# Hybrid decoder block on one core: seven-product gate and up tiles that sum in one PSUM bank

## Chip, cores and metric

One core of a Trainium2 chip runs the whole program in one launch. The metric is the device time in microseconds (us). TensorE (PE) does the matmuls, VectorE (DVE) and ScalarE (ACT) work beside it, GpSimd (POOL) does a little, and SyncE (SP) issues nearly all transfers. Results of matmuls land in PSUM, which has eight banks; everything else on the chip lives in SBUF.

## The reference

A decoder block on 512 tokens, with 16 learned tokens ahead of them (528 in all), model width 1024, in float32. A feed-forward network, a token mixer (latent attention and a gated DeltaNet out of one input projection), a second feed-forward network and a last norm:

```python
def swiglu(x, w_gate, w_up, w_down):
    return (jax.nn.silu(x @ w_gate) * (x @ w_up)) @ w_down
...
h = h + 0.5 * swiglu(rmsnorm(h, ffn1_norm[l]), ffn1_w_gate[l], ffn1_w_up[l], ffn1_w_down[l])
u = rmsnorm(h, mix_norm[l])
...
merged = jax.nn.sigmoid(gate_mla) * y_mla + jax.nn.sigmoid(gate_gdn) * y_gdn
h = h + merged @ w_out[l]
h = h + 0.5 * swiglu(rmsnorm(h, ffn2_norm[l]), ffn2_w_gate[l], ffn2_w_up[l], ffn2_w_down[l])
...
return rmsnorm(h, final_norm)[:, N_META:]
```

The hidden width of either network is 2816, which is 22 tiles of 128.

## The kernel before

Activations stand with the channels on the 128 partitions and the tokens along the row. A float32 product is made of three matmuls of the type fp32r: both sides are split into a high part (a cast by ACT: L173 for plain weights, L272 elsewhere) and a low part (the rest, a subtraction by DVE: L174, L273), and high x high, high x low and low x high are summed.

**The feed-forward networks** (`ffn`). The first six of the 22 hidden tiles are made by plain products, gate and up, "dense" in what follows (L188). The other 16 are made in pairs. For one pair and one of gate and up (a *quad*, j = 0 for gate and 1 for up; 16 quads per network, 32 in all) the two hidden tiles and the two halves of the tokens form a 2 x 2 block product, which is computed with seven instead of eight block products (the Winograd form of Strassen's method). `quad` loads the two raw weight tiles (512 KB each, in a pool of four), makes four sums of weight blocks on DVE (`side`, L394), splits each of the seven weight operands (`form`: 128x512 into one tile, high part in its first half and low part in its second, in eight slots of three kinds) and runs seven products (`product`, L405) of twelve matmuls each: four blocks of 128 channels times three. A matmul has 264 columns in FFN1 and 256 in FFN2. Every product has a PSUM bank to itself, from four small pools in the order of `BANKS`. After each product DVE adds it to a partial sum or to the output (`add`, L398; eight per quad); only the first product is copied by ACT (L421). The activation operands of the products, `xf`, are formed once per network.

The 22 hidden tiles stand in three chunks, `CHUNKS`: 0 to 8 (the six dense tiles and one pair), 8 to 16 and 16 to 22. In chunks 1 and 2 the down projections of the chunk before follow the quads: `down(c, m)` loads and splits one weight tile (L173, L174), runs 48 matmuls in FFN1 (two halves) or 24 of 512 columns in FFN2 (L188, tile `dn`), and DVE adds the result to the residual `hk` (L323). So chunk 1 is eight times quad and down, chunk 2 six quads with eight downs. At the end of a chunk, `halve` splits its hidden tiles for the downs to come (ACT cast into `ra`, L272). The downs of the last chunk follow at the end.

**The mixer** lies between the two networks. Its weights go through the same pool as the downs' (`wtiles`: `wraw`, `whi`, `wlo`, three slots each). What sets its order is a priority per part (`At`), by which a scheduler places the instructions on each engine.

**What sets the order around the change.** Each engine works through its own queue in the order that the scheduler wrote; it waits where an operand, or a slot that a tile is to reuse, is not ready. Products of a quad stand on PE in the order of the code: 1, 6, 2, 7, 5, 3, 4.

## Time and profile before

| what | us |
|---|---|
| median of three runs | 1211.47 |
| lowest, highest | 1210.93, 1213.09 |
| span of the profiled execution | 1213.2 |

The profiled execution is one more execution; its span lies 1.7 us above the median of the runs. Times in the views count from the start of that span. FFN1's dense tiles run until some 81 us, its quads until about 327 us and its last downs until 374 us; the mixer lasts until about 847 us; FFN2's quads follow from some 916 us, its last downs end about 1198 us. In a row of the views, L12 is line 12 of the kernel, `x84` a count of instructions, and "<-" in brackets names what ended the idle time ahead. PEclk is the clock that TensorE was granted, 1.00 being 2.4 GHz and 0.50 being 1.2 GHz.

### The profile page before, as it was taken

To read this page: it belongs to the slowest core of one execution; us is meant where nothing else is said; L and a number is where in the kernel's file an instruction comes from. 1 tells how busy PE (TensorE), PEld (TensorE's weight loads), DVE (VectorE), ACT (ScalarE), POOL (GpSimd) and SP (SyncE) were. 2 spreads that over 40 slices of the span, in tenths; PEclk is the share of its full clock that TensorE was granted. 3 is DMA by queue.
4 is the path that set the end of the run, shared out by engine and by line. 5 is a ranking of instruction groups with operands and counts; after the bars stand their busy time and mean duration, and the time that the engine had idled before them with its cause. 6 is when DMAs were issued, how large, how long until landed. Compare 5 with 4: busy or idle time off the path is not lost.

```text
span 1213.2 us, 20599 instructions
## 1 busy us (share of the span) xinstructions
PE 1182.6 (97%) x8094; PEld 1072.4 (88%) x8094; DVE 857.0 (71%) x1545; ACT 539.7 (44%) x922; POOL 127.1 (10%) x129
## 2 busy tenths in 40 slices
PE   7999999999999899999999999999999999999996
PEld 7999999999999789788897777788889999999985
DVE  7978777876656877784667665554979777786754
ACT  6544334533345553254425564434536433543443
POOL 1000000000011545020400000222000000000002
PEclk9999999999999888898999999999999999999998
DMA  6433233232244322245534544554642233233222
GB/s 233 143 103 100 94 105 105 88 118 75 88 138 138 126 61 81 81 145 149 162 101 142 173 132 135 169 185 141 199 157 88 90 103 104 94 106 115 79 78 70
DMA packets 68961, 145.37 MB, mean 120 GB/s; under 512 B 20000, under 2 KB 26480, under 8 KB 68864
## 3 DMA queue, kind: packets, MB, share of 16 engines
q1 hardware_dynamic: 68320, 143.52, 37.0%
q8 instruction: 64, 1.05, 0.3%
q10 hardware_dynamic: 544, 0.52, 0.1%
q14 instruction: 33, 0.27, 0.1%
HBM read 126.47 MB, written 17.55 MB: 119 GB/s over the span
## 4 chain that ended last, share of the span: by engine, by line
PE 86%; DVE 5%; issue 3%; POOL 2%; ACT 2%; DMA 2%; SPq 0%; DVEq 0%; POOLq 0%; ACTq 0%
PE gu L405 27%; PE dn L188 21%; PE gu L188 11%; PE gate L188 6%; PE wo L188 4%; PE mo L188 3%; PE qkv L188 2%; DVE wlo L174 1%; PE kk L804 1%; PE s L1085 1%; PE s L1082 1%; PE qk L943 1%; POOL rk L827 1%; DVE rk L827 1%; DVE T L829 1%
## 5 line engine op out<-in xcount | busy, mean ns | idle before, releaser
L173 ACT CAST whi<-wraw 128x1024 fp32r<-128x1024 f32 (+1 forms) x127 | 129.2, 1017 | 195.6 <-issue 65.3
L174 DVE TENSOR_TENSOR wlo<-wraw,whi 128x1024 fp32r<-128x1024 f32 (+1 forms) x127 | 155.8, 1227 | 26.2 <-ACT whi L173 25.5
L405 PE MATMUL gu<-hd,form 128*128 128x264 f32 (+1 forms) x1152 | 154.6, 283 | 0.0
L405 PEld LDWEIGHTS gu<-hd,form 128*128 128x128 f32 x1152 | 146.6, 190 | 1.3
L272 ACT CAST form<-sf 128x512 fp32r<-128x512 f32 x128 | 78.6, 620 | 126.1 <-DVE sf L394 67.5
L323 DVE SCALAR_TENSOR_TENSOR hk<-dn,hk 128x528 f32<-128x528 f32 (+2 forms) x49 | 33.7, 688 | 109.8 <-PE dn L188 109.6
L405 PE MATMUL gu<-ut,form 128*128 128x264 f32 x768 | 101.1, 284 | 0.0
L405 PE MATMUL gu<-rb,form 128*128 128x256 f32 x768 | 100.0, 283 | 0.0
L188 PE MATMUL dn<-hd,whi 128*128 128x264 f32 (+2 forms) x366 | 97.4, 319 | 0.0
L272 ACT CAST form<-wraw 128x512 fp32r<-128x512 f32 x96 | 59.3, 620 | 85.2 <-PE gu L405 52.1
L405 PEld LDWEIGHTS gu<-ut,form 128*128 128x128 f32 x768 | 96.5, 188 | 0.0
L405 PEld LDWEIGHTS gu<-rb,form 128*128 128x128 f32 x768 | 95.6, 192 | 0.0
L273 DVE TENSOR_TENSOR form<-sf,form 128x512 fp32r<-128x512 f32 x128 | 86.9, 683 | 11.2 <-ACT form L272 11.1
L188 PE MATMUL gate<-ut,whi 128*128 128x512 f32 x256 | 87.8, 417 | 0.0
L188 PE MATMUL dn<-ra,whi 128*128 128x264 f32 x464 | 85.3, 285 | 0.0
L188 PE MATMUL dn<-ut,whi 128*128 128x512 f32 (+1 forms) x238 | 83.6, 390 | 0.0
L235 POOL TENSOR_TENSOR sqa<-sq 128x512 f32<-128x512 f32 (+1 forms) x3 | 4.5, 1514 | 674.3 <-ACT sq L222 674.3
L188 PE MATMUL gu<-ra,whi 128*128 128x264 f32 x384 | 64.5, 290 | 7.4 <-ACT whi L173 6.6
L188 PE MATMUL dn<-ra,wlo 128*128 128x264 f32 x352 | 71.6, 285 | 0.0
L188 PE MATMUL dn<-ut,wlo 128*128 128x512 f32 (+1 forms) x182 | 70.4, 387 | 0.0
L273 DVE TENSOR_TENSOR form<-wraw,form 128x512 fp32r<-128x512 f32 x96 | 65.5, 684 | 6.7 <-ACT form L272 6.4
L188 PEld LDWEIGHTS dn<-ra,whi 128*128 128x128 f32 x464 | 68.5, 189 | 0.0
(435 smaller groups left out, 2480.7 us busy)
## 6 DMA issues: line engine op xcount, KB each, us to landing
wraw<-w SPq DMA_DIRECT2D x88, 512.0 KB, 3.3
wraw<-win SPq DMA_DIRECT2D x36, 512.0 KB, 3.5
wraw<-d SPq DMA_DIRECT2D x32, 512.0 KB, 3.8
wraw<-d SPq DMA_DIRECT2D x16, 384.0 KB, 3.2
hk<-xT SPq DMA_DIRECT2D x16, 264.0 KB, 3.6
dec<-growd SPq DMA_DIRECT2D x8, 512.0 KB, 5.8
gated<-gt SPq DMA_DIRECT2D x16, 256.0 KB, 2.2
sg<-gated SPq DMA_DIRECT2D x16, 256.0 KB, 2.8
```

Source lines behind the costliest of these rows:

```text
L173: ih = nc.scalar.copy(hi[:, 0:n], raw[:, 0:n])
L174: il = (nc.gpsimd if pool_lo else nc.vector).tensor_tensor(out=lo[:, 0:n], in0=raw[:, 0:n], in1=hi[:, 0:n].bitcast(F32), op=ALU.subtract)
L188: trail.append(nc.tensor.matmul(o, lhsT=w, rhs=x[:, lo_:hi_], start=start and k == 0 and pi == 0, stop=stop and k == n - 1 and pi == 2).ins)
L272: nc.scalar.copy(hi, x)
L273: (eng or nc.vector).tensor_tensor(out=lo, in0=x, in1=hi.bitcast(F32), op=ALU.subtract)
L323: nc.vector.scalar_tensor_tensor(out=o, in0=p, scalar=0.5, in1=o, op0=ALU.mult, op1=ALU.add)
L405: nc.tensor.matmul(ps, lhsT=wt, rhs=xt, start=k == 0 and i == 0, stop=k == 3 and i == 2)
L804: nc.tensor.matmul(ps[0:n, h4, 0:n], lhsT=hs(kT, h, o, o + n), rhs=hs(kT, h, o, o + n), start=True, stop=True)
L827: eng.tensor_tensor(out=tm, in0=lt[:, m + 1:m + 1 + n, m:m + 1].broadcast_to([nl, n, m + 1]), in1=T[:, m:m + 1, 0:m + 1].broadcast_to([nl, ...
L829: eng.tensor_tensor(out=T[:, m + 1:m + 1 + n, 0:m + 1], in0=T[:, m + 1:m + 1 + n, 0:m + 1], in1=tm, op=ALU.subtract)
L943: nc.tensor.matmul(ps[:, h4], lhsT=hs(kT, h, o, o + n), rhs=hs(qT, h, o, o + n), start=True, stop=True)
L1082: nc.tensor.matmul(ps[:, 0:w], lhsT=Q[h][:, b * P:(b + 1) * P], rhs=K[h][:, k0:k1], start=True, stop=True)
```

## The change

`quad` is written anew; products, operands and results are the same up to signs.

- **Banks.** Bank A takes products 1, 6, 7 and 4 one on top of the other: only product 1 starts a new sum. Between them ACT copies the partial sum out (`p1` after product 1, `u2` after 6, `u3` after 7). Bank B takes product 2. Bank C takes product 5 and, after that has been read, product 3, from zero each. Since only sums can be made in this way, some signs are turned: two of the activation operands, the output that takes product 5 and the one that is left in A are negated by a multiplication with -1 in the instruction that reads them. The output in A is read from the bank itself, by the silu (gate) or by the multiplication with the gate (up).
- **Order of products.** Products 4 and 3 of a quad are put off (`late`) into the next quad: product 1, 2, the old 4, 6, the old 3, 5, 7, then the down. At the end of a chunk `flush` places them around a down that is held back.
- **Weights.** The two raw tiles become one tile of 16 blocks, 1 MB, in two buffers; the second load writes its two halves to either end of it. The four sums are one instruction of 1024 columns and two of 512, all additions. The operands are split in blocks of eight (1024 columns), in pairs `whi`/`wlo` from the same pool as the downs' and the mixer's; that pool has four slots each instead of three, everywhere. `form` and its eight slots are no longer used.
- **Settings.** `NCP` 3 to 4, `NSF` 3 to 2 (larger tiles), and a smaller scratch area for transfers that software describes.

PE has the same number of matmuls; DVE has 1307 instructions instead of 1547, ACT 878 instead of 894. The old `quad` stands in the listing above and is left out of the diff.

```diff
-NCP = 3
-NRAW = 4
-NSF = 3
+NCP = 4
+NRAW = 2
+NSF = 2
 ORD = (2, 0, 3, 1, 4, 5, 6, 7)
 ONP = (2, 3)
-NFORM = {"whi": 3, "wlo": 3, "wex": 2}
+NFORM = {"whi": 4, "wlo": 4}
...
-            hi = wp.tile([P, 8, P], F32R, tag="whi", name="whi")
-            lo = wp.tile([P, 8, P], F32R, tag="wlo", name="wlo")
+            hi = wp.tile([P, 8, P], F32R, tag="whi", name="whi", bufs=NFORM["whi"])
+            lo = wp.tile([P, 8, P], F32R, tag="wlo", name="wlo", bufs=NFORM["wlo"])
...
-                for o, p, q in ((x[:, lhs], x[:, rhs], x[:, lhs]), (x[:, rhs], y[:, rhs], x[:, rhs]),
-                                (y[:, rhs], y[:, rhs], x[:, lhs]), (y[:, lhs], y[:, lhs], y[:, rhs])):
-                    nc.vector.tensor_tensor(out=o, in0=p, in1=q, op=ALU.subtract)
+                nc.vector.tensor_tensor(out=x[:, lhs], in0=x[:, lhs], in1=x[:, rhs], op=ALU.subtract)
+                nc.vector.tensor_tensor(out=x[:, rhs], in0=y[:, rhs], in1=x[:, rhs], op=ALU.subtract)
+                for o, q in ((y[:, rhs], x[:, lhs]), (y[:, lhs], y[:, lhs])):
+                    nc.vector.scalar_tensor_tensor(out=o, in0=y[:, rhs], scalar=-1.0, in1=q, op0=ALU.mult, op1=ALU.subtract)
...
-            def product(p, ps, w):
-                f = form(w, hid)
+            banks = [0]
+            def side(tag, x, y):
+                return nc.vector.tensor_tensor(out=tag, in0=x, in1=y, op=ALU.add)
+            def halves_of(t, n):
+                hi = wp.tile([P, 8, P], F32R, tag="whi", name="whi", bufs=NFORM["whi"])
+                lo = wp.tile([P, 8, P], F32R, tag="wlo", name="wlo", bufs=NFORM["wlo"])
+                split(wp, t, hi[:, 0:n], lo[:, 0:n])
+                return [(hi[:, k], lo[:, k]) for k in range(n)]
+            def product(p, ps, w, first, last):
                 for k in range(4):
-                    xh, xl = xf[p][k]
-                    for i, (wt, xt) in enumerate(((f[:, k], xh), (f[:, k], xl), (f[:, 4 + k], xh))):
-                        nc.tensor.matmul(ps, lhsT=wt, rhs=xt, start=k == 0 and i == 0, stop=k == 3 and i == 2)
-            def quad(ft, j, o0, o1):
...
+                    (wh, wl), (xh, xl) = w[k], xf[p][k]
+                    for i, (wt, xt) in enumerate(((wh, xh), (wh, xl), (wl, xh))):
+                        nc.tensor.matmul(ps, lhsT=wt, rhs=xt, start=first and k == 0 and i == 0, stop=last and k == 3 and i == 2, skip_group_check=True)
+            late = []
...
+            def flush(n=2):
+                for _ in range(n):
+                    if late:
+                        late.pop(0)()
+            def quad(ft, j, o0, o1, end):
+                raw = hid.tile([P, 16, P], F32, tag="wq", name="wq", bufs=NRAW)
+                nc.sync.dma_start(raw[:, 4:12], wg[ft, j])
+                nc.sync.dma_start(raw.rearrange("p (a b) x -> p a b x", a=4)[:, 0:4:3], wg[ft + 1, j].rearrange("p (a b) x -> p a b x", a=2))
+                s31 = hid.tile([P, 8, P], F32, tag="sf", name="sf", bufs=NSF)
+                s24 = hid.tile([P, 8, P], F32, tag="sf", name="sf", bufs=NSF)
+                a21, a11, a12, a22 = (raw[:, 4 * i:4 * i + 4] for i in range(4))
+                f1 = halves_of(raw[:, 4:12], 8)
+                nc.vector.tensor_tensor(out=s31.rearrange("p (a b) x -> p a b x", a=2), in0=a21.unsqueeze(1).broadcast_to([P, 2, 4, P]),
+                                        in1=raw.rearrange("p (a b) x -> p a b x", a=4)[:, 1:4:2], op=ALU.add)
+                nc.vector.tensor_tensor(out=s24[:, 0:4], in0=s31[:, 4:8], in1=a11, op=ALU.add)
+                nc.vector.tensor_tensor(out=s24[:, 4:8], in0=s24[:, 0:4], in1=a12, op=ALU.add)
+                c1, c2 = (tmp.tile([P, NT], F32, tag="cp", name="cp", bufs=NCP)[:, 0:n] for _ in range(2))
+                p1, u2, u3 = c1[:, lhs], c1[:, rhs], c2[:, lhs]
+                A = sm_tile("gua")[:, 0:h]
+                B = mm_tile("gub")[:, 0, 0:h]
+                banks[0] ^= 1
+                C = (tk_tile if banks[0] else ax_tile)("guc")[:, 0:h]
+                product(1, A, f1[0:4], True, True)
+                nc.scalar.copy(p1, A)
+                product(2, B, f1[4:8], True, True)
+                nc.vector.tensor_tensor(out=o0[:, lhs], in0=B, in1=p1, op=ALU.add)
+                flush(1)
+                f3 = halves_of(s24, 8)
+                product(6, A, f3[0:4], False, True)
+                nc.scalar.copy(u2, A)
+                flush(1)
+                f2 = halves_of(s31, 8)
+                product(5, C, f2[4:8], True, True)
+                product(7, A, f2[0:4], False, True)
+                nc.scalar.copy(u3, A)
+                nc.vector.scalar_tensor_tensor(out=o1[:, rhs], in0=C, scalar=-1.0, in1=u3, op0=ALU.mult, op1=ALU.subtract)
+                f4 = halves_of(a22, 4)
+                def last_a():
+                    product(4, A, f4, False, True)
+                    end(1, lhs, A)
+                def last_c():
+                    product(3, C, f3[4:8], False, True)
+                    nc.vector.tensor_tensor(out=o0[:, rhs], in0=C, in1=u2, op=ALU.add)
+                    end(0, slice(0, n), None)
+                    end(1, rhs, None)
+                late.extend((last_a, last_c))
...
-                        quad(ft, j, *os)
-                        for i, o in enumerate(os):
+                        def end(i, t, ps, j=j, os=os, gs=gs):
+                            o = os[i][:, t]
                             if j == 0:
-                                table(o, o, AF.Silu)
+                                table(o, o if ps is None else ps, AF.Silu, scale=1.0 if ps is None else -1.0)
+                            elif ps is None:
+                                nc.vector.tensor_tensor(out=o, in0=o, in1=gs[i][:, t], op=ALU.mult)
                             else:
-                                nc.vector.tensor_tensor(out=o, in0=o, in1=gs[i], op=ALU.mult)
+                                nc.vector.scalar_tensor_tensor(out=o, in0=ps, scalar=-1.0, in1=gs[i][:, t], op0=ALU.mult, op1=ALU.mult)
+                        quad(ft, j, *os, end)
                         q += 1
-                        if c:
-                            while given < KT * q // nq:
-                                down(c - 1, given)
-                                given += 1
+                        while c and given < KT * q // nq - (q == nq):
+                            down(c - 1, given)
+                            given += 1
+                flush(1)
+                while c and given < KT:
+                    down(c - 1, given)
+                    given += 1
+                flush(1)
...
-    nc = bacc.Bacc("TRN2", target_bir_lowering=False, num_devices=1)
+    nc = bacc.Bacc("TRN2", target_bir_lowering=False, num_devices=1, dynamic_dma_scratch_size=4096)
```

The order on the engines, in three places. First the end of chunk 0 in FFN1, where the last quad of the chunk meets the first of chunk 1. On ACT, before; `p1` is the copy of product 1, `ra` the split of a hidden tile, `whi` the first down's weights:

```order
L272 CAST form_1315<-sf_1312 128x512
L272 CAST form_1368<-sf_1310 128x512
L272 CAST form_1351<-sf_1348 128x512
L272 CAST form_1388<-sf_1385 128x512
L173 CAST whi_1424<-wraw_1423 128x1024
L272 CAST ra_1275<-hd_977 128x528
L421 COPY p1_1292<-gu_1293 128x264
```

and after (`cp` is a partial sum out of bank A, `gua`; `gua_1087` is the last quad of chunk 0, `gua_1273` the first of chunk 1):

```order
L272 CAST whi_1302<-sf_1263 128x1024
L445 COPY cp_1086<-gua_1087 128x264
L272 CAST whi_1319<-sf_1262 128x1024
L272 CAST whi_1349<-wq_1259 128x512
L272 CAST ra_1251<-hd_978 128x528
L434 COPY cp_1271<-gua_1273 128x264
L173 CAST whi_1354<-wraw_1353 128x1024
L272 CAST ra_1247<-hd_977 128x528
L440 COPY cp_1271<-gua_1273 128x264
```

One copy of a quad became three, and casts became half as many of twice the width; a copy now stands behind such a cast (whi_1302) or behind two casts and `ra`. On PE, at the same place, before: the last product of a quad, a bank of its own, and the next quad's product 1 on another:

```order
L405 MATMUL gu_1232<-ut_969,form_1233 128x264
L405 MATMUL gu_1232<-ut_970,form_1233 128x264
L405 MATMUL gu_1232<-ut_969,form_1233 128x264
L405 MATMUL gu_1293<-hd_893,form_1294 128x264 x3
L405 MATMUL gu_1293<-hd_914,form_1294 128x264 x3
L405 MATMUL gu_1293<-hd_935,form_1294 128x264 x3
```

and after: eleven matmuls of the new quad's product 1, and then the old quad's product 4 on its bank A, `gua_1087`, behind product 7 on that bank:

```order
L404 MATMUL gua_1273<-hd_893,whi_1264 128x264 x2
L404 MATMUL gua_1273<-hd_893,wlo_1265 128x264
L404 MATMUL gua_1273<-hd_914,whi_1264 128x264 x2
L404 MATMUL gua_1273<-hd_914,wlo_1265 128x264
L404 MATMUL gua_1273<-hd_935,whi_1264 128x264 x2
L404 MATMUL gua_1273<-hd_935,wlo_1265 128x264
L404 MATMUL gua_1273<-hd_956,whi_1264 128x264 x2
L404 MATMUL gua_1087<-ut_906,whi_1191 128x264
L404 MATMUL gua_1087<-ut_907,whi_1191 128x264
```

So product 4 no longer has other products between itself and product 7, only these eleven matmuls.

Second, ACT in a quad of chunk 1 with its down, before:

```order
L421 COPY p1_1486<-gu_1487 128x264
L173 CAST whi_1618<-wraw_1617 128x1024
L272 CAST form_1686<-wraw_1679 128x512
L272 CAST form_1724<-wraw_1679 128x512
L272 CAST form_1707<-sf_1704 128x512
L272 CAST form_1760<-sf_1702 128x512
L272 CAST form_1743<-sf_1740 128x512
L272 CAST form_1780<-sf_1777 128x512
L173 CAST whi_1816<-wraw_1815 128x1024
```

and after:

```order
L272 CAST whi_1651<-sf_1599 128x1024
L434 COPY cp_1607<-gua_1609 128x264
L272 CAST whi_1683<-sf_1598 128x1024
L272 CAST whi_1713<-wq_1595 128x512
L440 COPY cp_1607<-gua_1609 128x264
L173 CAST whi_1718<-wraw_1717 128x1024
L272 CAST whi_1780<-wq_1775 128x1024
L445 COPY cp_1608<-gua_1609 128x264
```

The seven casts of 512 became three of 1024 and one of 512; the copies `cp` stand between them; the down's cast (whi_1718) comes after the copy of `u2`, and the next quad's first cast after that.

Third, DVE in the mixer, in the middle of it, as a difference (the lines of the kernel after stand 23 higher there, so that a row with + often has its partner with - further on; `xt` is a transposed piece of the triangular systems, `rsq` and `rk` belong to the norms of queries and keys):

```order
+L879 STREAM_TRANSPOSE xt<-tb 128x512
 L204 TENSOR_SCALAR rsq<-ssq 128x256
+L1036 COPY kn<-kn 128x528
+L894 TENSOR_SCALAR nz<-z_6447 32x512 x2
+L208 SCALAR_TENSOR_TENSOR rsq<-rsq 128x256
+L1047 COPY v<-v 128x512
+L209 SCALAR_TENSOR_TENSOR rk<-rsq,rk 128x256
+L204 TENSOR_SCALAR rsq<-ssq 128x256
+L907 COPY t_6445<-x_6492 32x16x32
 L208 SCALAR_TENSOR_TENSOR rsq<-rsq 128x256
 L209 SCALAR_TENSOR_TENSOR rk<-rsq,rk 128x256
-L856 STREAM_TRANSPOSE xt<-tb 128x512
```

`xt` moved from behind the pieces of `rsq` and `rk` to ahead of them, and what waits for it (`nz`, the copies into `t`) with it; up to this place the mixer's order is as before.

## Rows read from the trace of the kernel before

**Rows 1.** The page's head and its first section: busy us, share, instructions

```profile
span 1213.2 us, 20599 instructions
...
PE 1182.6 (97%) x8094; PEld 1072.4 (88%) x8094; DVE 857.0 (71%) x1545; ACT 539.7 (44%) x922; POOL 127.1 (10%) x129
```

**Rows 2.** Windows by stage: us, then PE PEld DVE ACT POOL busy, PEclk, DMA

```profile
81.00:112.00 31.00, 31.00 (x258) 31.00 (x257) 30.78 (x59) 16.26 (x29) 0.00 (x0) 1.00 0.32 103
112.00:330.00 218.00, 218.00 (x1793) 218.00 (x1792) 160.29 (x282) 87.16 (x139) 0.00 (x0) 1.00 0.30 96
...
374.00:847.00 473.00, 460.16 (x2914) 388.16 (x2913) 305.29 (x601) 211.90 (x403) 102.20 (x104) 0.96 0.42 132
...
950.00:1155.00 205.00, 205.00 (x1412) 190.74 (x1411) 154.18 (x273) 84.80 (x135) 0.00 (x0) 1.00 0.31 100
```

**Rows 3.** Chain that ended last, FFN1 and FFN2: start, us, engine, line

```profile
117.76 10.22 PE gu L405 x84
127.98 5.85 PE dn L188 x48
...
967.23 10.07 PE gu L405 x84
977.30 5.58 PE dn L188 x24
```

**Rows 4.** PE's waits, whole run: line, releaser, us in total, times, longest

```profile
PE z L188 <- ACT whi L173: 1.0, 1, 1.0
...
PE z L864 <- DVE xt L856: 0.4, 1, 0.4
```

**Rows 5.** DVE's groups, 112 to 328 us: count | busy, mean ns | idle before

```profile
L273 DVE TENSOR_TENSOR form<-sf,form 128x512 fp32r<-128x512 f32 x52 | 35.4, 684 | 5.3 <-ACT form L272 5.3
...
L174 DVE TENSOR_TENSOR wlo<-wraw,whi 128x1024 fp32r<-128x1024 f32 x15 | 18.3, 1221 | 7.0 <-ACT whi L173 6.9
L394 DVE TENSOR_TENSOR sf<-wraw 128x512 f32<-128x512 f32 x24 | 16.4, 684 | 4.6 <-DMA wraw<-w 4.5
L398 DVE TENSOR_TENSOR cp<-gu,cp 128x264 f32<-128x264 f32 x26 | 11.0, 424 | 1.0 <-PE gu L405 1.0
...
L460 DVE TENSOR_TENSOR ra<-ra,g 128x528 f32<-128x528 f32 x8 | 5.6, 699 | 0.0
```

**Rows 6.** ACT's groups, the same stretch

```profile
L272 ACT CAST form<-sf 128x512 fp32r<-128x512 f32 x51 | 31.5, 621 | 48.6 <-DVE sf L394 28.1 <-PE gu L405 16.2 <-PE dn L188 4.3
...
L173 ACT CAST whi<-wraw 128x1024 fp32r<-128x1024 f32 x15 | 15.8, 1052 | 26.7 <-issue 15.3 <-PE dn L188 11.4
L147 ACT ACTIVATE g<-g 128x528 f32<-128x528 f32 x13 | 8.4, 643 | 1.3 <-DVE g L398 1.3
L421 ACT COPY p<-gu 128x264 f32<-128x264 f32 x13 | 4.9, 379 | 8.2 <-PE gu L405 8.0
L272 ACT CAST ra<-ra 128x528 fp32r<-128x528 f32 x8 | 4.9, 633 | 0.9 <-PE dn L188 0.5
```

**Rows 7.** Timeline of PE, second product of a quad in chunk 1: start, us

```profile
215.50 1.64 PE L405 MATMUL gu<-ut,form 128*128 128x264 f32 x12
```

**Rows 8.** Timeline of ACT, copy of that quad's first product

```profile
215.69 0.38 ACT L421 COPY p<-gu 128x264 f32<-128x264 f32 x1 [1.08 <-PE gu L405]
```

**Rows 9.** DMA issues, gate and up weights: KB each, median us to landing

```profile
wraw<-w SPq DMA_DIRECT2D x88, 512.0 KB, 3.3
```

**Rows 10.** Timeline of ACT in the mixer: a cast, idle before and releaser

```profile
514.57 1.05 ACT L173 CAST whi<-wraw 128x1024 fp32r<-128x1024 f32 x1 [4.51 <-PE z L188]
```

**Rows 11.** Timeline of DVE in the mixer

```profile
542.54 0.68 DVE L249 TENSOR_TENSOR sqa<-sq 128x512 f32<-128x512 f32 x1
...
547.14 0.70 DVE L856 STREAM_TRANSPOSE xt<-tb 128x512 f32<-128x512 f32 x1
```

**Rows 12.** Windows of 5 us in the mixer, columns as in Rows 2

```profile
550.00:555.00 5.00, 5.00 (x68) 4.17 (x68) 2.54 (x4) 2.43 (x6) 0.00 (x0) 0.60 0.40 147
555.00:560.00 5.00, 5.00 (x19) 3.97 (x17) 3.11 (x4) 2.52 (x5) 0.00 (x0) 0.50 0.29 91
```

More of the change, by code (lines that the diff above doesn't have):

```diff
@@ L385, in ffn @@
                     xf[p].append((hi, lo))
-            def m0_tile(name):
-                return mm_tile(name)[:, 0, :]
-            PT = [{"m": m0_tile, "s": sm_tile, "t": tk_tile, "a": ax_tile}[c] for c in BANKS]
-            def side(x, y, op=ALU.subtract):
-                t = hid.tile([P, 4, P], F32, tag="sf", name="sf", bufs=NSF)
-                nc.vector.tensor_tensor(out=t, in0=x, in1=y, op=op)
-                return t
-            def add(o, x, y):
-                nc.vector.tensor_tensor(out=o, in0=x, in1=y, op=ALU.add)
@@ L400, in product @@
-            def product(p, ps, w):
-                f = form(w, hid)
-                for k in range(4):
-                    xh, xl = xf[p][k]
-                    for i, (wt, xt) in enumerate(((f[:, k], xh), (f[:, k], xl), (f[:, 4 + k], xh))):
-                        nc.tensor.matmul(ps, lhsT=wt, rhs=xt, start=k == 0 and i == 0, stop=k == 3 and i == 2)
-            def quad(ft, j, o0, o1):
-                raw = []
-                for i in range(2):
-                    nraw[0] += 1
-                    raw.append(hid.tile([P, 8, P], F32, tag="wrx", name="wraw", bufs=NRAW - 3) if nraw[0] % NRAW >= 3
-                               else wp.tile([P, 8, P], F32, tag="wraw", name="wraw", bufs=3))
-                for i in range(2):
-                    nc.sync.dma_start(raw[i], wg[ft + i, j])
-                a11, a12, a21, a22 = raw[0][:, 0:4], raw[0][:, 4:8], raw[1][:, 0:4], raw[1][:, 4:8]
-                c1 = tmp.tile([P, NT], F32, tag="cp", name="cp", bufs=NCP)[:, 0:n]
-                u2, u3 = c1[:, lhs], c1[:, rhs]
-                p1 = tmp.tile([P, HALF], F32, tag="p1", name="p1", bufs=2)[:, 0:h]
-                ps = PT[0]("gu")[:, 0:h]
-                product(1, ps, a11)
-                nc.scalar.copy(p1, ps)
-                s1 = side(a21, a22, ALU.add)
-                s2 = side(s1, a11)
-                ps = PT[1]("gu")[:, 0:h]
-                product(6, ps, s2)
-                add(u2, ps, p1)
-                ps = PT[2]("gu")[:, 0:h]
-                product(2, ps, a12)
-                add(o0[:, lhs], ps, p1)
-                s3 = side(a11, a21)
-                ps = PT[3]("gu")[:, 0:h]
-                product(7, ps, s3)
-                add(u3, ps, u2)
-                ps = PT[4]("gu")[:, 0:h]
-                product(5, ps, s1)
-                add(o1[:, rhs], ps, u3)
-                add(u2, ps, u2)
-                s4 = side(a12, s2)
-                ps = PT[5]("gu")[:, 0:h]
-                product(3, ps, s4)
-                add(o0[:, rhs], ps, u2)
-                ps = PT[6]("gu")[:, 0:h]
-                product(4, ps, a22)
-                add(o1[:, lhs], ps, u3)
@@ L446, in ffn @@
-            todo = []
+            banks = [0]
[7 more added lines that the diff above has]
+            def product(p, ps, w, first, last):
+                for k in range(4):
+                    (wh, wl), (xh, xl) = w[k], xf[p][k]
+                    for i, (wt, xt) in enumerate(((wh, xh), (wh, xl), (wl, xh))):
+                        nc.tensor.matmul(ps, lhsT=wt, rhs=xt, start=first and k == 0 and i == 0, stop=last and k == 3 and i == 2, skip_group_check=True)
```

## The prediction, made before the kernel after was run

> **What bounds the kernel now.** I began with the page. The span is 1213.2 us and TensorE is busy for 1182.6 us of it, 97% [rows 1]; what else a busy share of 97% hides has to be read by stage. In the table of windows [rows 2] PE's busy time equals the length of the stretch, at clock 1.00, in all three stretches that the change edits: 81 to 112 us (last two quads of chunk 0 of FFN1 and their neighbours), 112 to 330 us (chunks 1 and 2) and 950 to 1155 us (FFN2). In 81 to 112 us DVE is also busy for 30.78 of 31 us, and PE still loses nothing. The chain of waits [rows 3] says the same as a rhythm: 84 matmuls of L405 take 10.22 us (121.7 ns each), then a down projection of 48 takes 5.85 us (121.9 ns each), and in FFN2 84 take 10.07 us and 24 wide ones 5.58 us. There is no gap between the pieces. The sum of PE's waits over the whole run [rows 4] has no row with L405 in it. What PE loses (473.00 less 460.16 = 12.84 us [rows 2]) it loses in the mixer.
>
> **Part by part.**
>
> *The products.* 32 quads of seven products of twelve matmuls are 2688 matmuls before and after, in the same shapes. Could one cost less or more when it accumulates on an earlier product in bank A, or reads its halves from two tiles? The down projections do both, 24 matmuls into one bank out of separate whi and wlo, and take 121.9 ns against 121.7 ns [rows 3]. So 0, and no gain below it: PE has no idle time there to give.
>
> *Fewer sums, larger splits.* Per quad DVE does four sums of 684 ns, seven lo halves of 685 ns, eight adds of 425 ns [rows 5], half of a pair of multiplications of 699 ns, plus 1.22 us for the down's lo half and, for its accumulation, 0.7 us like the multiplication of the same width: 10.9 + 0.7 + 1.9 = 13.5 us of a period of 10.22 + 5.85 = 16.07 us. Afterwards: one 1024-wide sum (bound 1.22 us by the lo half of that size, the nearest row), two of 684 ns, lo halves of 3 x 1.22 + 0.69, three adds of 0.43 and some 0.8 of multiplications: 8.3 + 0.8 + 1.9 = 11 us. ACT's share stays: 7 x 0.62 + 0.38 + 0.64 + 1.05 = 6.4 us before, 3 x 1.05 + 0.62 + 3 x 0.38 + 0.64 + 1.05 = 6.6 us after [rows 6]. Both lie beside a PE that is full: 0. If that cover were gone, the 2.5 us of a quad would be worth at most 32 x 2.5 = 80 us, but no row shows PE waiting for DVE there.
>
> *The new waits in a steady quad.* Products 6, 7 and 4 write bank A, so each must wait for ACT's copy out of it. An ACT copy starts 0.19 us after the next product has begun (215.50 to 215.69 [rows 7, 8]) and takes 0.38 us. By the order after, PE runs product 1, 2, the old 4, 6, the old 3, 5, 7, so between product 1 and 6, and between 6 and 7, lie two others: 2 x 1.46 = 2.92 us. Even with a cast of 1.05 us ahead in ACT's queue the copy is out after 0.19 + 1.05 + 0.38 = 1.62 us. Covered: 0.
>
> *The weights of the down projection.* The pairs whi/wlo now have four slots for the four tiles of a quad and for the down's. Counted from product 1, the down's cast gets the slot of the old product 3, free at 5 x 1.46 = 7.30 us: cast 7.5 to 8.55, lo half until about 9.8 (10.1 if another DVE piece is ahead). PE first wants that lo half at 10.22 + 4 x 0.122 = 10.71 us in FFN1 and at 10.07 + 2 x 0.23 = 10.53 us in FFN2. The margin is about 0.4 to 0.9 us: 0 taken, but this is the narrowest place.
>
> *The ends of chunks.* There the spacing is lost. At chunk 0 to 1 product 4 follows 11 matmuls after product 7, at 1 to 2 likewise 11 of the down: 11 x 0.122 = 1.34 us. ACT has a cast of 1.05 us ahead of the copy: 0.19 + 1.05 + 0.38 + some 0.05 = 1.67 us, so PE waits about 0.3 us. At 0 to 1 the next copy of product 1 stands behind a cast of 0.62 and ra of 0.63 us [rows 6], and product 6 may wait 0.4 us. Per FFN 0.3 + 0.3 + 0.4 = 1.0 us, both **+2.0 us**; bounds 0 (casts early) to +4 (a second cast of 1.05 us ahead at the four places). At the last chunk's end a whole down lies between: 0.
>
> *Raw weights.* One tile of 1 MB in two buffers replaces four of 0.5 MB; the load of the quad after the next can start when the old product 4's split is done, more than 8 us before its use, and a load lands in 3.3 us [rows 9]. 0.
>
> *Start, mixer, tail.* At the start one lo half moves behind a short sum on DVE, while PE is full from 20 us on; the tail's order is the same: 0. In the mixer the fourth slot lets a cast go early that stood 4.51 us behind PE [rows 10], where PE then waited for it 1.0 us [rows 4]: -1.0, bounds -1.0 and 0. Beyond 540 us DVE's xt moves from behind the rsq and rk pieces (547.14 us) to right behind sqa (542.54 + 0.68 = 543.2 us) [rows 11]; PE waited 0.4 us for it [rows 4]: -0.4. Together **-1.4 us**. But matmuls of that part are reordered too, and its clock is not steady: 0.60 and 0.50 in the ten us from 550 us [rows 12]. At full speed that would save (1 - 0.60) x 5 + (1 - 0.50) x 5 = 4.5 us; a second such stretch would cost as much. I take 0 for the clock and keep both ends.
>
> *Sum.* 0 + 2.0 - 1.4 = +0.6 us. On the profiled span 1213.2 + 0.6 = 1213.8 us; that span is 1.7 us over the median of the runs, so **1211.5 + 0.6 = about 1212.0 us** for the median.
>
> **A rule against the change.** In the kernel before every product has a bank of its own, so no row shows a product waiting until another engine has read its bank. The Trainium skill, page "PSUM — Partial Sum Buffer", section "PSUM bank collisions raise a hardware error", says that TensorE and a reading engine must not touch one bank of the same partitions at once. By that rule none of the copies can overlap the next product on A, and three waits per quad are real; if nothing were between them, each would cost the full copy. What they cost here is the sum of the rows above: covered in a quad, uncovered at chunk ends.
>
> **Rivals.**
>
> *Slower: the down's lo half comes late in every quad.* Place: the 14 quads with a down in each FFN, 28 in all. It decides where slot, cast and lo half together pass 10.7 us (10.5 in FFN2), that is, when DVE has more than 0.4 to 0.9 us ahead of that lo half; one 1.22 us half of the next quad is enough. Price 0.2 to 0.4 us x 28 = 6 to 11 us: 1218 to 1223 us. For it: DVE works through long pieces now, and a queue cannot be overtaken. Against: DVE has 5 us to spare per quad. If only the chunk ends are worse (+4 and no gain in the mixer), it ends at 1215.5 us. Together 0.25.
>
> *Faster: the mixer's clock.* The reordered stretch around 545 to 562 us keeps the full clock: -4.5 - 1.4 + 2.0 = -3.9, 1207.6 us; without the waits at chunk ends 1205.6 us. For it: PE ran 4.62 of 5 us in 545 to 550 us with 32-wide matmuls in it, and then fell to half [rows 12], and these are exactly what moves. Against: such stretches stand in other parts of the mixer that do not move (mean clock 0.96 over 473 us [rows 2]). 0.20. The Trainium skill, "TensorE: Matmul & The Clock Gate", Part 1, says that the throttled state is the default and recent activity releases it; the rows agree in so far as the clock falls although PE stands as busy, with small matmuls. [...]
>
> *The change does not do what it says.* The deferred products or copies could be put elsewhere by the scheduler; the order shows them as written, so this has its place only in the chunk ends above.
>
> **How the numbers follow.** Forecast 0.55: sum between -1.4 (no waits) and +2.6 (no mixer gain, waits +2.6), 1210 to 1214 us. Slower 0.25, faster 0.20. About 0.2%, or 2.4 us, is what a measurement of this kernel can tell from no change, so faster means under 1209.1 and slower above 1213.9 us. The range leaves out the far half of either rival: low 1206.5, from the middle of the faster case, and high 1218.0, from the low end of the late lo half.
>
> **What would show it.** Right: PE gapless in the quads, 84 matmuls still in 10.2 us; waits of L404 (the product's line after) for the copies of L434 to L445 only at four places, 0.3 to 0.4 us each; DVE's busy time in the FFN stretches lower by some 2.5 us a quad, 60 to 80 us in all; PE's wait for whi at 515 us gone. Wrong: a row of PE waiting for wlo before dn, 14 times per FFN (the slower rival); a cadence other than 121.7 ns; or the stretch from 550 us at clock 1.00 (the faster one), or new half-clock stretches elsewhere.

## The result and the profile after

The kernel after takes 1220.84 us (median of 8 runs) beside 1212.28 us for the kernel before, measured together: a ratio of 1.0082, 95% interval 1.0057 to 1.0107. A second measurement (e3 below) gave 1.0047, 1.0027 to 1.0068. By the two ratios it is slower by 6 to 10 us; the forecast was 1212.0 us, with 1218.0 us as the upper end.

The page's head and the windows by stage of the kernel after, columns as in [rows 1] and [rows 2]:

```profile
span 1219.1 us, 20179 instructions
...
PE 1184.7 (97%) x8094; PEld 1071.6 (88%) x8094; DVE 813.8 (67%) x1305; ACT 549.2 (45%) x906; POOL 130.4 (11%) x129
```

```profile
81.00:112.00 31.00, 30.99 (x253) 30.75 (x253) 25.05 (x35) 15.93 (x26) 0.00 (x0) 1.00 0.32 108
112.00:330.00 218.00, 218.00 (x1786) 217.78 (x1785) 140.58 (x183) 91.67 (x135) 0.00 (x0) 1.00 0.28 90
...
374.00:847.00 473.00, 457.15 (x2904) 384.38 (x2903) 302.60 (x598) 210.29 (x400) 104.11 (x104) 0.96 0.41 131
...
950.00:1155.00 205.00, 205.00 (x1402) 189.96 (x1401) 136.98 (x180) 87.30 (x131) 0.00 (x0) 1.00 0.29 93
```

In the networks PE is as full as before (99.97% in 81 to 112 us, all of the other two stretches) and DVE has less to do: 857.0 us became 813.8 us over the whole run. In 374 to 847 us PE is busy for 457.15 us instead of 460.16. PE's waits (line, releaser, us in total, times, longest), where [rows 4] stood before:

```profile
PE yT L991 <- DVE zs L992: 2.1, 2, 1.3
...
PE x L902 <- ACT X L909: 0.8, 1, 0.8
PE z L188 <- DVE z L616: 0.8, 1, 0.8
PE yT L991 <- DVE bv L986: 0.6, 1, 0.6
...
PE qk L966 <- DVE bv L937: 0.6, 1, 0.6
```

The waits of z for whi and for xt are gone; in their place stand z for its own earlier tile, x, qk and above all yT, the transposes at the end of the DeltaNet scan. Cut into stages by the first matmul of each, the profiles give (us; two each of before and after):

| stage | before | before, e4 | after | after, e3 |
|---|---|---|---|---|
| first product to the mixer's first matmul (FFN1) | 292.36 | 292.36 | 293.64 | 293.65 |
| mixer, first part, up to the matmuls kn | 166.24 | 164.36 | 167.51 | 164.12 |
| mixer, second part, kn to the merge (mo) | 218.52 | 216.46 | 220.87 | 220.31 |
| first product of FFN2 to its last down | 285.67 | 285.69 | 286.28 | 286.32 |

(FFN2's last down of the kernel before ends at 1201.3 us of its span, not at about 1198.) So the networks lose 1.3 and 0.6 us, the tail behind FFN2 some 0.35 us, and most of the rest of the loss stands in the second part of the mixer, which begins where the order was moved. The first part varies with its half-clock stretches, in either kernel.

The level of before needs a word: in the 19 profiled executions of this record that have both, the time lies 1.7 to 2.1 us above the span. The profiled execution of before, with a span of 1213.2 us, took therefore about 1215 us, more than the median; e4's span is 1209.3 us at a mean clock of 0.986, and e3, the kernel after at the same 0.986, has 1215.2 us: 5.9 us between them.

### The profile page after: what moved, and what is told of

Same layout as the page of the kernel before. It is cut to its first block, busy times and chain, and to the rows that moved or that the text cites. A ratio compares the mean times of both kernels' runs of the same rounds, so it can differ in the third digit from the quotient of the medians.

```text
span 1219.1 us, 20179 instructions
## 1 busy us (share of the span) xinstructions
PE 1184.7 (97%) x8094; PEld 1071.6 (88%) x8094; DVE 813.8 (67%) x1305; ACT 549.2 (45%) x906; POOL 130.4 (11%) x129
## 4 chain that ended last, share of the span: by engine, by line
PE 87%; DVE 6%; POOL 2%; DMA 2%; issue 1%; ACT 1%; SPq 0%; DVEq 0%; POOLq 0%; ACTq 0%
PE dn L188 21%; PE gua L404 15%; PE gu L188 11%; PE guc L404 8%; PE gate L188 7%; PE gub L404 4%; PE wo L188 4%; PE mo L188 3%; PE qkv L188 2%; DVE wlo L174 1%; DMA wraw<-w 1%; PE kk L827 1%; PE s L1108 1%; PE pt L1147 1%; PE z L188 1%
## 5 line engine op out<-in xcount | busy, mean ns | idle before, releaser
L272 ACT CAST whi<-sf 128x1024 fp32r<-128x1024 f32 x64 | 67.2, 1050 | 136.7 <-PE dn L188 83.6
L273 DVE TENSOR_TENSOR wlo<-sf,whi 128x1024 fp32r<-128x1024 f32 x64 | 78.4, 1225 | 18.7 <-ACT whi L272 17.5
L273 DVE TENSOR_TENSOR wlo<-wq,whi 128x1024 fp32r<-128x1024 f32 x64 | 61.1, 954 | 35.9 <-ACT whi L272 35.6
L272 ACT CAST whi<-wq 128x1024 fp32r<-128x1024 f32 x64 | 53.5, 835 | 65.5 <-PE gua L404 33.9
L404 PE MATMUL gua<-ut,whi 128*128 128x264 f32 x384 | 72.0, 285 | 0.0
L404 PE MATMUL gua<-rb,whi 128*128 128x256 f32 x384 | 70.9, 284 | 0.0
L188 PE MATMUL qkv<-ut,whi 128*128 128x264 f32 x384 | 66.8, 293 | 0.0
L188 PEld LDWEIGHTS dn<-hd,whi 128*128 128x128 f32 x366 | 61.1, 189 | 4.7 <-DVE hd L273 0.5
L188 PEld LDWEIGHTS gu<-ra,whi 128*128 128x128 f32 x384 | 54.5, 192 | 8.4 <-ACT whi L173 6.6
L404 PEld LDWEIGHTS gua<-rb,whi 128*128 128x128 f32 x384 | 59.9, 192 | 0.7 <-ACT cp L445 0.6
```

Of the source, the lines that this page charges most:

```text
L188: trail.append(nc.tensor.matmul(o, lhsT=w, rhs=x[:, lo_:hi_], start=start and k == 0 and pi == 0, stop=stop and k == n - 1 and pi == 2).ins)
L272: nc.scalar.copy(hi, x)
L273: (eng or nc.vector).tensor_tensor(out=lo, in0=x, in1=hi.bitcast(F32), op=ALU.subtract)
L404: nc.tensor.matmul(ps, lhsT=wt, rhs=xt, start=first and k == 0 and i == 0, stop=last and k == 3 and i == 2, skip_group_check=True)
```

## Experiments

**Which half of the change: e1 to e4.** e1 is the kernel before with the four slots alone:

```diff
-NFORM = {"whi": 3, "wlo": 3, "wex": 2}
+NFORM = {"whi": 4, "wlo": 4, "wex": 2}
-            hi = wp.tile([P, 8, P], F32R, tag="whi", name="whi")
+            hi = wp.tile([P, 8, P], F32R, tag="whi", name="whi", bufs=NFORM["whi"])
```

(likewise `wlo`, and the smaller scratch area). e2 is the kernel after with three slots:

```diff
-NFORM = {"whi": 4, "wlo": 4}
+NFORM = {"whi": 3, "wlo": 3, "w4": 2}
             def halves_of(t, n):
+                if n == 4:
+                    hi = hid.tile([P, 4, P], F32R, tag="w4h", name="w4h", bufs=NFORM["w4"])
...
```

> The kernel before with its old quads, and only the pool of split weights with four slots of each half instead of three (and the smaller scratch area that makes room). The order of the mixer then is the one of the kernel after, matmul for matmul. Theory 'mixer order' (the fourth slot lets the scheduler place the mixer differently, and that costs 6 to 8 us): 1217 to 1221 us against about 1212 for before; the profile shows waits of the yT matmuls near 645 us. Rival 'new quads' (the seven-product tiles are what costs): within 2 us of before.

> The new quads of the kernel after, but three slots again for the split weights; product 4's operand, half as wide, gets two slots of its own in the networks. The mixer's order is that of the kernel before, matmul for matmul. Theory 'mixer order': before plus about 2 us (waits at the ends of chunks), 1213 to 1215 us, mixer as long as before. Rival 'new quads': as slow as the kernel after, 1219 to 1222 us.

> The kernel after, unchanged, for a second profile beside the others on one chip. Both theories: 1219 to 1222 us. If the half-clock stretches in the mixer lie elsewhere than in the first profile, they are chance of an execution; if again near 645 us, they belong to the order.

> The kernel before, unchanged, for a second profile. The first one had a span of 1213.2 us. If what lies outside the span is 1.8 us, as in the kernel after, that execution took 1215 us, some 3 us over the median, and a typical span is 1210 to 1211 us with fewer half-clock stretches in the mixer.

Measured, against the same runs of before: e1 1219.83 us, ratio 1.0063 (1.0035 to 1.0090); e2 1213.61 us, 1.0007 (0.9982 to 1.0033); e3 1219.39 us, 1.0047; e4 1212.47 us, 0.9999. The four slots alone, with the old quads, cost as much as the whole change; the new quads with three slots end where before does. That is a balance and not nothing twice: in e2's profile the quads begin 1.2 us later than in e4's, the networks take 2.3 us more, and the second part of the mixer, in the order of before, takes 2.7 us less. This part, one window from kn to mo each, of e4 (before), of e3 (after), of e1 and of e2:

```profile
537.89:754.35 216.46, 214.25 (x1493) 173.18 (x1491) 130.18 (x291) 103.76 (x226) 22.24 (x21) 0.99 0.46 145
```

```profile
538.85:759.16 220.31, 215.69 (x1493) 173.58 (x1491) 129.47 (x291) 103.32 (x225) 23.29 (x21) 0.99 0.46 143
```

```profile
539.26:762.24 222.98, 217.27 (x1493) 175.05 (x1492) 130.73 (x291) 103.41 (x225) 23.73 (x21) 0.98 0.46 141
```

```profile
539.92:753.70 213.78, 212.48 (x1493) 172.25 (x1492) 130.31 (x291) 103.29 (x224) 22.25 (x21) 1.00 0.48 147
```

The idle time of PE is 2.21 us in before, 4.62 us in after, 5.71 us in e1 and 1.30 us in e2. The busy time differs as well: 214.25, 215.69, 217.27 and 212.48 us, at mean clocks of 0.99, 0.99, 0.98 and 1.00.

**Why four slots cost: e5 to e8.** The fourth slot lets SP load the query weights `uq` (and `ukv` ahead of them) one place earlier; qr and qn then stand earlier on PE, and gate matmuls, which fill PE beside the scan, are left for later: 96 of them stand between kn and the first yT, where e4 has 105. At the end of the scan yT comes in four groups, with 3 gate matmuls between them where e4 has 8. PE's timeline at the first three in the kernel after, and the windows of 5 us around it:

```profile
643.90 0.66 PE L991 MATMUL yT<-ident,bv 128*128 128x128 f32 x4 [0.63 <-DVE bv L986]
...
646.24 1.11 PE L991 MATMUL yT<-ident,bv 128*128 128x128 f32 x4 [1.27 <-DVE zs L992]
648.14 1.12 PE L991 MATMUL yT<-ident,bv 128*128 128x128 f32 x4 [0.78 <-DVE zs L992]
```

```profile
640.00:645.00 5.00, 4.21 (x22) 2.68 (x20) 4.13 (x14) 4.41 (x15) 0.00 (x0) 1.00 0.28 76
645.00:650.00 5.00, 2.98 (x14) 2.50 (x14) 4.78 (x10) 0.00 (x0) 0.00 (x0) 0.58 0.70 192
650.00:655.00 5.00, 5.00 (x23) 4.11 (x24) 3.11 (x10) 1.75 (x5) 0.00 (x0) 0.73 0.48 155
```

A group waits until DVE has read the single bank of the group before (`zs`). PE is idle for 2.8 us in 640 to 650 us, and in 645 to 655 us the clock is granted at 0.58 and 0.73. In before no such wait is listed. e5 gives yT the pool with two banks, e8 one with two double banks; e6 and e7 move the query weights to later priorities:

```diff
-                ps = tk_tile("yT").rearrange("p (i t) -> p i t", i=4)
+                ps = sm_tile("yT").rearrange("p (i t) -> p i t", i=4)
...
-            with At(WPRI):
+            with At(18):
                 wq = weights(a["uq"][:, 0:8], 8) + weights(a["uq"][:, 8:12], 4)
```

(the first pair is e5, with `mm_tile("yT")[:, 0]` it is e8; the second is e6, with `At(51)` it is e7).

> The kernel after with one word changed in the mixer: the four transposes yT take their PSUM bank from the pool of two banks instead of the single one, so that a group need not wait until DVE has read the bank of the group before. PE's order is the same up to that place; there gate matmuls now stand between the groups. Theory 'yT' (PE idle at 640 to 650 us behind DVE's zs, and the half clock that follows, are the loss): 3 to 5 us less than the kernel after, no yT wait and clock 1.00 around 645 us. Rival 'early queries' (the loss is spread over the whole reordered stretch): within 1.5 us of the kernel after.

> The kernel after, with the load and split of the query weights (uq) given a later priority, so that they come behind one more gate weight. The matmuls qr and qn then stand later, and yT is spread among gate matmuls. Theory 'yT': 3 to 5 us less than the kernel after. Rival 'early queries': also less, so this run alone tells only that the early uq is the switch; it tells both from 'four slots in themselves', by which it would be as slow as the kernel after.

> As e6, with the query weights at the priority of the queries themselves, later still: qn stands in a row after the scan, and gate matmuls around yT. Theory 'yT': 3 to 5 us less than the kernel after, but qn in one row may leave the heads of the attention waiting; up to 2 us of that lost again. 'Four slots in themselves': as slow as the kernel after.

> The kernel after with yT's bank from the pool of two double banks, where scores and projections also live: eleven gate matmuls ahead of yT and four or three between the groups, scores later. Theory 'yT': 3 to 5 us less than the kernel after, as in e5. Rival 'early queries': within 1.5 us of the kernel after.

Measured: e5 1215.69 us, ratio 1.0037 (1.0007 to 1.0066); e6 1230.45 us, 1.0140 (1.0109 to 1.0170); e7 1221.06 us, 1.0062; e8 1221.27 us, 1.0063. Only e5 went the way the theory of yT had it, 4 to 5 us under the kernel after by its median; but its ratio stands only 0.0010 under that of e3, well inside the intervals, so the gain isn't shown. e7 and e8 are as slow as after: in e8 the yT waits are gone, but a gate matmul waits 2.8 us for DVE at the same place, and in e7 z and gates wait, 1.9 and 2.4 us. PE's listed waits between 535 and 772 us sum up to 3.9, 5.3, 4.3 and 4.5 us in e5 to e8, beside 4.4 in e3 and 2.0 in e4. So yT is where PE waits in the order of after, but neither it nor the early uq is the one switch: each of these orders waits somewhere. e6 was a plain miss. Its windows:

```profile
585.00:590.00 5.00, 3.19 (x37) 2.57 (x37) 3.02 (x4) 3.59 (x9) 0.77 (x2) 0.81 0.57 166
590.00:595.00 5.00, 5.00 (x24) 3.60 (x22) 1.94 (x4) 0.45 (x2) 1.32 (x2) 0.50 0.49 135
...
605.00:610.00 5.00, 5.00 (x19) 4.02 (x19) 2.74 (x8) 1.06 (x1) 1.50 (x2) 0.50 0.14 35
```

A matmul of the triangular systems (x) waits 1.8 us for ACT until 587.83 us, and from then on PE runs at half clock until past 610 us, although it is busy all the time. The second part of the mixer takes 230.16 us, 9.9 us more than in e3, far more than the gap itself. A like stretch followed gaps of about 1 us in the profiles of e5, e10 and e11. The gap alone doesn't bring it: in e3 the same matmul waits 0.8 us, and the clock stays. The Trainium skill, "TensorE: Matmul & The Clock Gate", Part 1, says that the throttled state is the default and activity releases it; these rows agree that the clock falls behind a gap, but they also show it staying down while PE is busy with small matmuls of the scan and gate matmuls of 512 columns between them.

**The ends of chunks: e9, e10.** e9 lets the next chunk's first quad take the late products and splits the hidden tiles after it; e10 doesn't put them off at all:

```diff
                         quad(ft, j, *os, end)
+                        for t in todo:
+                            halve(t)
...
+                if c < len(CHUNKS) - 1:
...
+                    todo.extend(range(k0, k1))
+                    continue
```

```diff
                 late.extend((last_a, last_c))
+                flush()
```

> The kernel after, with the put-off products 4 and 3 of the last quad of chunks 0 and 1 left to the next chunk's first quad like all others (the hidden tiles of the chunk are split after that quad). Product 4 then has products 1 and 2 ahead of it instead of eleven matmuls. The mixer's order stays that of the kernel after. If the waits at chunk ends are what the networks lost: the stretch from the first L404 to the mixer's first matmul falls from 293.6 by 0.5 to 0.7 us, toward the 292.4 us of before; if the rest of the loss is something else, 0.5 us stays. In the whole time 1 us less than the kernel after, which these runs can hardly tell.

> The kernel after, with products 4 and 3 run at the end of their own quad, right behind product 7. If a product on bank A has to wait for the whole copy (0.19 + 0.38 us, and a cast of up to 1.05 us ahead of it in ACT's queue), PE waits 0.6 to 1.6 us in each of 32 quads: 18 to 50 us more than the kernel after. If copy and product could overlap on one bank: no wait, the same time.

Measured: e9 1217.78 us, ratio 1.0063 (1.0034 to 1.0093); FFN1's stretch is 292.81 us and FFN2's 285.71 us, that is, 0.83 of 1.28 us and all of the 0.6 us come back. e10 1228.43 us (two runs), with FFN1 at 296.64 and FFN2 at 288.34 us: 3.0 and 2.1 us more than after, not 18 to 50. The scheduler put eleven matmuls of the down between product 7 and product 4 by itself, as at the chunk ends, so that under 0.2 us a quad is left of the waits (5.1 us over 32 quads). (Most of the rest of the profiled execution's time is the mixer at half clock.) So e10 doesn't tell what a product right behind product 7 would have cost.

**Both mended: e11 to e14.** e11 is e9 and e5 together; e12 is e9 and e2 together; e13 and e14 also hold back the first raw loads of the quads, which had stood ahead of dense weights:

```diff
-                nc.sync.dma_start(raw[:, 4:12], wg[ft, j])
+                loads.append(nc.sync.dma_start(raw[:, 4:12], wg[ft, j]))
+                if n == NT and len(loads) < 3:
+                    behind(loads[-1].ins, dense[HB[len(loads) - 1]])
```

(`dense` are the casts of the dense weights, `HB` is (6, 8) in e13 and (7, 9) in e14).

> e9 and e5 together: the kernel after with spaced chunk ends and two banks for yT. 4 to 6 us less than the kernel after, that is 1214 to 1216 us beside 1212 to 1214 for before: still no gain, since PE was full in the networks of before and the mixer's reordered middle part keeps some 2 us of loss.

> e9 and e2 together: the new quads with spaced chunk ends, the mixer in the order of before. Theory 'mixer order plus chunk ends': within 1.5 us of before. If DVE's relief of some 44 us were worth anything to the whole, this would be faster than before by more than 2.4 us.

> e12, with the first raw loads of the first two quads held until the seventh and the ninth dense weight is split, so that they no longer stand ahead of dense weights in SP's queue (in e12 the quads begin 1.2 us late, behind a wait of the dense stage). Theory: quads begin at 81.2 instead of 82.5 us, the mixer in the order of before, chunk ends without wait: 1 us less than e12, 0 to 3 us less than before. Rival 'the mixer's order is not all, the networks' new quads cost more than their trace shows': e12's time or more.

> As e13, held until the eighth and the tenth dense weight. The same as e13 within 1 us, if the loads then still land before the quads begin; a wait of the first quad for its loads if not.

Measured: e11 1214.77 us, ratio 1.0020 (0.9998 to 1.0043); e12 1210.29 us, 0.9993 (0.9976 to 1.0010); e13 1209.38 us, 0.9985 (0.9959 to 1.0012); e14 1208.70 us, 0.9971 (0.9954 to 0.9987). e14 is faster than the kernel before, by 0.3%; e13, which differs only in the two places of the loads, can't be told from it. The networks are no part of that gain (292.80 and 285.72 us, 0.5 us more than before): it lies in the mixer's second part, 213.31 us, in the very order of before. e11 can be told neither from before nor from e9, so the two banks of yT aren't shown to mend the loss.

**Where e14's gain comes from: e15 to e18.** SP's timeline at the three tb transfers, of before and of e14, and two windows of e14 where before had [rows 12]:

```profile
536.15 2.24 SPq L855 DMA_DIRECT2D tb<-td  x3
```

```profile
534.77 1.32 SPq L895 DMA_DIRECT2D tb<-td  x3
```

```profile
545.00:550.00 5.00, 4.78 (x100) 3.93 (x99) 4.56 (x9) 3.94 (x11) 0.00 (x0) 1.00 0.62 214
550.00:555.00 5.00, 5.00 (x81) 4.16 (x79) 3.61 (x6) 3.59 (x7) 0.00 (x0) 1.00 0.40 122
```

In before the issue of the three takes 2.24 us, in e14 1.32 us; ACT's copy of tb follows 3.45 and 2.38 us behind the first issue, and PE's clock holds where it fell in before. That the one brings the other is argued from their order in time and not shown. All six profiles of this mixer's order with the old quads have 2.2 to 2.7 us there, all four with the new quads 1.32 us. In the former a packet of the instruction queue starts at the first of the three (536.33 us in before), in e14 only at 540.82 us. The slow issue goes with the packet: there stands e14's last tb transfer, whose issue takes 1.74 us, and without the packet 0.43 us in before:

```profile
543.05 0.43 SPq L855 DMA_DIRECT2D tb<-td  x1
```

```profile
540.87 1.74 SPq L895 DMA_DIRECT2D tb<-td  x1
```

The same holds in all ten profiles: this issue takes 1.07 to 1.74 us in the four with the packet beside it, and 0.43 or 0.44 us in the six without. e15 and e16 shift SP's instructions in the kernel before by two and four small transfers at the start, e17 and e18 those of DVE, ACT and GpSimd by eight and twenty:

```diff
             nc.sync.dma_start(triu, a["triu"])
+            for _ in range(2):
+                nc.sync.dma_start(cst.tile([P, 1], F32, tag="pad", name="pad"), a["cols"][:, 0:1])
```

> The kernel before with two transfers of 512 bytes more at the start of SP's queue, into a tile that nothing reads; all else, order included, is as before. In the two profiles of before the issue of the three tb transfers near 536 us took 2.24 to 2.30 us, with a packet of the instruction queue beside it, and the clock fell behind it; in the kernels with the new quads and the mixer's old order it took 1.32 us without such a packet, and the clock stayed. Theory 'place of the instruction fetch': the additional transfers shift SP's instructions, the three issues take 1.32 us, the stretch from 545 to 562 us runs at clock 1.00, and the whole is 2 to 4 us less than before, as e14. Rival 'the new quads bring it' (DVE's relief or another placement of data): 2.24 us again and the time of before.

> As e15 with four such transfers, for the case that two don't shift the fetch out of the tb issues. Theory 'place of the instruction fetch': 1.32 us and 2 to 4 us less than before in at least one of the two. Rival: the time of before in both.

> The kernel before with eight tiny instructions more on each of DVE, ACT and GpSimd at the start, on tiles that nothing reads; the order of the rest is as before. If the instruction packet beside the tb issues (536 us in before, 540.5 us in e14) belongs to one of these three queues, it moves, the three issues take 1.32 instead of 2.24 us, and the clock holds from 545 to 562 us: 2 to 4 us less than before. If it belongs to PE or SP, or if it only chances to stand there, it stays at the first tb issue, with 2.2 us and the time of before.

> As e17 with twenty tiny instructions on each of the three engines instead of eight: the same alternatives with the same times, for the case that eight are too few to move the packet out of the tb issues.

Measured: e15 1213.17 us, ratio 1.0011; e16 1212.51 us, 1.0012; e17 1213.43 us, 1.0006; e18 1212.02 us, 1.0005; every interval holds 1. The packet stayed at the first tb issue in all four, and the three issues took 2.22, 2.26, 2.74 and 2.42 us. What places the packet isn't settled, then, nor whether it is the cause of the slow issue or only stands beside it; PE's own instructions were not shifted. The rival in e15's expectation, that the new quads bring the gain by DVE's relief or by another placement of data, is left standing.

## Why the prediction was wrong, step by step

- **The products, 0: right.** A steady quad still takes 10.22 us, from the end of one down to the start of the next:

```profile
109.48 5.88 PE dn L188 x48
125.58 5.87 PE dn L188 x48
```

  L404 shows nowhere in the list of waits; but neither do the waits at the chunk ends below, of 0.1 to 0.3 us, so the rhythm is the better sign. (The prediction puts all of PE's idle time in the mixer; of the 30.6 us in before the mixer has 12.84, and the rest lies at the start and in the tail.)
- **DVE's relief, 0: right in its worth, wrong in its size.** The pieces cost what they were priced at; 112 to 328 us of DVE in the kernel after:

```profile
L273 DVE TENSOR_TENSOR wlo<-sf,whi 128x1024 fp32r<-128x1024 f32 x26 | 31.8, 1225 | 5.0 <-ACT whi L272 4.3
...
L423 DVE TENSOR_TENSOR sf<-wq 128x1024 f32<-128x1024 f32 x12 | 14.7, 1225 | 0.4
```

  But the whole fell by 43 us, not by 60 to 80: over the 13.6 quads of 112 to 330 us DVE was busy for 11.8 us each before (160.29 / 13.6, not 13.5) and is for 10.3 after (140.58 / 13.6, not 11). The sum added up mean durations, and in the records neighbouring instructions of DVE overlap: in this window their durations add up to 177.4 us before and 147.0 us after, 17.1 and 6.4 us more than the busy time. Fewer, longer instructions overlap less, so part of the forecast relief was that overlap. e2 and e12 have the relief without the order, at 1.0007 and 0.9993.
- **Waits in a steady quad and the down's lo half, 0: right.** PE never waits for it; the slower rival that was written out did not happen.
- **Ends of chunks, +2.0: right in place, a little large.** e9 takes back 1.4 us. The wait at chunk 0 to 1, on PE and on ACT:

```profile
99.84 0.41 PE L404 MATMUL gua<-hd,whi 128*128 128x264 f32 x2
100.25 0.51 PE L404 MATMUL gua<-ut,whi 128*128 128x264 f32 x2
```

```profile
98.88 1.05 ACT L272 CAST whi<-sf 128x1024 fp32r<-128x1024 f32 x1 [1.37 <-PE gua L404]
99.84 0.37 ACT L445 COPY cp<-gua 128x264 f32<-128x264 f32 x1
```

  Product 4 starts at 100.25 us, right behind the end of the copy (99.84 + 0.37); product 4 takes 1.73 us to the start of the next instead of 1.46, so that 0.27 us are lost; the forecast had 0.3. The second place has as much, product 6's wait was 0.1 us and not 0.4. The Trainium skill, "PSUM — Partial Sum Buffer", section "PSUM bank collisions raise a hardware error", says that TensorE must not write a bank while another engine reads it; the two rows agree, 0.04 us apart. Of the 0.45 us that stay in FFN1 in e9, about half are in the downs (129.24 us in all, 129.01 in before) and the rest in the quads; why, no run tells.
- **The mixer, -1.4: this step failed.** The whole mixer came out 3.6 us longer in either pair of profiles (before and after, e4 and e3), and e1 shows it alone. The -1.0 for the fourth slot did not come: the cast still waits for PE as in [rows 10],

```profile
517.17 1.05 ACT L173 CAST whi<-wraw 128x1024 fp32r<-128x1024 f32 x1 [4.51 <-PE z L188]
```

  and z now waits 0.8 us for DVE. The -0.4 of xt came. So the term came out at +3.6 us instead of -1.4. What was not looked at is everything behind that: the order of the 220 us after the first moved row. It was in the order at hand that uq, qr and qn moved ahead, that gates moved behind, and that yT stood on one bank with less between its groups; the sum took all of this as zero, with the clock as its only risk. e1 shows that the slots bring the loss; which of the moved pieces makes it up stays open, since e5 to e8 took none of it back that their intervals can tell. Of e3's 3.9 us over e4 in the second part, 2.4 are idle time (4.62 less 2.21), as much as PE waits between the groups of yT, and 1.4 busy time at the same mean clock, which no run explains.
- **The clock rival: half right.** The stretch of [rows 12] did keep its clock in the kernel after, as that rival had it, and time was lost again at 645 us:

```profile
550.00:555.00 5.00, 5.00 (x89) 4.21 (x86) 3.39 (x7) 1.78 (x5) 0.00 (x0) 1.00 0.42 156
```

  That the clock is down while PE stands as busy, in [rows 12] and for longer in e6, is no agreement with a release by activity, as the prediction has it.
- **The level.** The profiled execution was taken as 1.7 us above the median; it was some 3.

## What to carry to other kernels

A buffer count in a shared pool is a change of the order wherever the pool is used; split it from the rest of a change first, as e1 and e2 do. Where a scheduler moves instructions, follow the moved stretch to its end, for the work that fills PE beside a serial chain: after the move it may stand elsewhere than where the chain waits. Where PE is full, a lighter DVE bought nothing here. And a sum of mean durations is more than the busy time where instructions overlap.

## What the runs showed of the hardware

A gap of PE of 1.8 us ahead of small matmuls was followed by some 24 us at the 1.2 GHz level (e6), with PE busy throughout; after the waits at 645 us in the kernel after, of 2 us together, the clock came back within 10 us. The time of this kernel follows its mean clock: runs of before range from 1206 us at 0.991 to 1217 us at 0.980. The issue of three transfers of 32 KB in SP's queue took 1.32 us, or 2.2 to 2.7 us with a packet of the instruction queue beside it; the two profiles of before agree (2.24 and 2.30 us), so it goes by the program rather than by chance.
